# Chunk scans of an RWKV-7 layer: inverses a batch ahead from small products of their own, two heads per masked product, undecayed state, fixed order

## The chip, the core and the metric

The kernel runs on one core of a Trainium2 chip. TensorE (PE in the profile, its weight loads PEld) multiplies matrices out of SBUF into PSUM, VectorE (DVE), ScalarE (ACT) and GpSimd (POOL) work on tiles, and SyncE (SP) issues most of the DMAs. The metric is the device time of one execution in microseconds (us).

## The reference

One encoder layer over 1024 tokens of width 1024, in float32: a norm and one wide projection; banded attention with 8 query heads; an RWKV-7 time mix with 8 heads of 64, as a forward and a backward scan whose outputs are added; gates, an output projection, and a feed-forward part. The scan is what the change is about:

```python
def step(state, inp):
    r_t, w_t, k_t, v_t, a_t, b_t = inp
    sa = jnp.einsum('dbhij,dbhj->dbhi', state, a_t)
    state = (state * w_t[..., None, :] + sa[..., :, None] * b_t[..., None, :]
             + v_t[..., :, None] * k_t[..., None, :])
    y = jnp.einsum('dbhij,dbhj->dbhi', state, r_t)
    return state, y
```

The attention takes 128 queries at a time against three blocks of 128 keys, with a softmax that has one extra logit per head.

## The kernel before

The scan is done by chunks: 16 chunks of 64 tokens (NCH), two directions (ND, the backward one takes the chunks from the end), 8 heads, which lie as four pairs (NP) of two heads in 128 partitions, and two groups of four heads (g). The stage ahead of attention writes to DRAM, for each direction and chunk, `ra_d` (for each head 64 columns of the decayed a and 64 of the decayed r) and `bk_d` (64 columns of b and 64 of k, with b first for the forward direction), and `v_d`.

For one chunk and direction, `products` (L869) multiplies bk by ra for each head, which gives a 128x128 matrix, and masks it into `gm` on VectorE. The rows of b against the columns of a are a strictly triangular 64x64 matrix L, and the scan needs the inverse of I - L. A batch is four chunks (NB), so 4 x 8 heads x 2 directions, 64 matrices. `inverse` (L892) does their 32x32 diagonal blocks at once on VectorE: transposes into `Lp`, then 31 pairs of a multiplication into `tmp` and an addition into `Z`, then two transposes into `Zn` and `Zt`; ScalarE puts these back into `gm`. `inverse_off` (L925) makes the off-diagonal blocks with 32x32 matmuls (`qps`) and puts them into `gm` as well. `gm` has two batches, in turn.

A step of the scan (one chunk, both directions) is then a chain: `w_part` (L979: `wps`, from v and from the old state `Sb`), a copy to `Wt`, `u_part` (L997: `ups`, the inverse times Wt), a copy to `UV`, `s_part` (L1006: `sps`, the state sums; `Tc` is the sum with the decayed old state `Sc`, and `Sb` is Tc times the decay `Dt` of the chunk), beside it `operands` (L957) for the next step, which transposes bk (`tmps`) into `tm`, and `y_part` (L1025: `yps`, the outputs).

What stands on TensorE between these is filler: `gates(0)` in the stages ahead of the scan (384 matmuls `gmm` of 128x512), and `beside` (L747: `gates(1)`, 384 more of the same, then the attention's up-projection, `uaps`) in the scan. `fill(n)` (L776) issues n matmuls of it, and the tables `FILL` and `WARM` say how many at which place; `ahead` says which later chunks' `products` go into which step. Only the masked products and the first matmul of the off-diagonal blocks are held in the order of the program. Everything else is put in an order by the framework's scheduler when the kernel is built: on each engine by the priority of the program's order and by when the scheduler takes an operand to be ready. That order is then fixed, and an engine that comes to an instruction whose operand is late waits.

The first four chunks' products, the first inverse and the first off-diagonal blocks come ahead of the first step. The attention (L674 to L735) is ahead of the scan: scores `sc` for a head, mask and maximum (`smk`), exponential on ScalarE, a scaling on VectorE (L718), transposes of the scores (`pt`, L721), copies to `pT`, and the output product `po` (L729).

## Time and profile before

| | |
|---|---|
| median of 3 runs | 1876.3 us (1874.92 to 1877.21) |
| the profiled execution's own time | 1880.39 us |
| its span | 1878.3 us |
| mean granted TensorE clock | 0.967 |
| attention | about 371 to 497 us of the span |
| chunk scans | about 498 to 938 us |

The profile is of one execution, and its times count from the start of the span. A busy matmul is longer in the records than its share of the stream, since the matmuls are pipelined: the distance from one start to the next says what one costs. fp32 matmuls stand in the trace twice, as two passes; in the listings of the order they stand once.

### The profile page before, as it was taken

How to read it: one execution, taken by the hardware profiler on the slowest of the kernel's cores; microseconds unless marked ns; L12 is line 12 of the kernel's file. 1: busy time of each engine (PE TensorE's matmuls, PEld its weight loads, DVE VectorE, ACT ScalarE, POOL GpSimd, SP SyncE). 2: the span in 40 equal slices, each digit the busy share in tenths (PEclk: the TensorE clock that was granted, in tenths of full speed). 3: DMA queues.
4: the chain of work that ended last, by engine and by line, in shares of the span. 5: the costliest groups of instructions: out<-in, count | busy, mean ns of one | idle time of the engine just before them, and what ended most of it. 6: DMA issues, size and time to landing. Idle time of an engine off the chain costs nothing.

```text
span 1878.3 us, 30687 instructions
## 1 busy us (share of the span) xinstructions
PE 1751.7 (93%) x11800; PEld 1409.7 (75%) x11800; DVE 1206.6 (64%) x2086; ACT 790.6 (42%) x1447; POOL 353.5 (19%) x330
## 2 busy tenths in 40 slices
PE   7999888989996999999978989999999999999998
PEld 7977666756675666666757987788787888888998
DVE  6646776667365668577795277676765786685432
ACT  5536666455423132314562144443443444454221
POOL 3444444521321122133243000000000000000000
PEclk9999999999998889999999999999999999999999
DMA  6362434752462444466557213545345984564111
GB/s 202 91 173 88 141 119 141 215 163 85 124 202 87 151 137 141 149 192 189 158 179 238 83 57 116 169 144 160 129 155 190 308 262 138 185 214 137 60 40 46
DMA packets 259603, 279.74 MB, mean 149 GB/s; under 512 B 15744, under 2 KB 178432, under 8 KB 259328
## 3 DMA queue, kind: packets, MB, share of 16 engines
q1 hardware_dynamic: 251200, 264.46, 44.7%
q0 software_dynamic: 7824, 12.59, 2.4%
q8 instruction: 93, 1.52, 0.3%
q10 hardware_dynamic: 432, 0.73, 0.1%
q14 instruction: 54, 0.44, 0.1%
HBM read 196.97 MB, written 80.74 MB: 148 GB/s over the span
## 4 chain that ended last, share of the span: by engine, by line
PE 40%; DVE 17%; DMA 6%; issue 4%; ACT 2%; SPq 1%; POOL 0%; DVEq 0%; POOLq 0%; ACTq 0%
PE ff2ps L1549 16%; DMA w1st<-in_w_ff_dram 4%; DVE w1l L175 2%; DVE Z L913 2%; PE ff1ps L1309 2%; DVE tmp L910 2%; PE plps L211 2%; PE plps L210 2%; PE plps L209 2%; PE gps L883 2%; PE mmo L209 2%; PE mmo L211 2%; PE mmo L210 2%; DVE h L1326 1%; DVE Sb L1021 1%
## 5 line engine op out<-in xcount | busy, mean ns | idle before, releaser
L175 POOL TENSOR_TENSOR wlo<-wst,whi 128x512 fp32r<-128x512 f32 (+1 forms) x116 | 182.1, 1583 | 332.6 <-ACT whi L174 316.1
L1549 PE MATMUL ff2ps<-th,sh 128*128 128x512 f32 x448 | 174.1, 390 | 3.6 <-ACT th L174 3.6
L1549 PE MATMUL ff2ps<-th,sl 128*128 128x512 f32 x448 | 175.2, 391 | 0.0
L1549 PE MATMUL ff2ps<-tl,sh 128*128 128x512 f32 x448 | 175.1, 391 | 0.0
L162 POOL TENSOR_TENSOR rstd<-ms,neghalf 128x1 f32<-128x1 f32 x24 | 13.3, 554 | 813.5 <-DVE ms L160 813.5
L174 ACT CAST whi<-wst 128x512 fp32r<-128x512 f32 (+1 forms) x116 | 73.5, 649 | 118.3 <-PE gmm L199 48.0
L174 ACT CAST sh<-sst 128x512 fp32r<-128x512 f32 x109 | 67.8, 622 | 113.5 <-PE ff2ps L1549 64.4
L197 PE MATMUL gmm<-hh,whi 128*128 128x512 f32 x256 | 110.1, 430 | 1.6 <-ACT gth L271 1.6
L201 PE MATMUL gmm<-hh,wlo 128*128 128x512 f32 x256 | 109.6, 428 | 0.0
L199 PE MATMUL gmm<-hl,whi 128*128 128x512 f32 x256 | 109.5, 428 | 0.0
L175 DVE TENSOR_TENSOR sl<-sst,sh 128x512 fp32r<-128x512 f32 x109 | 75.2, 689 | 52.2 <-ACT sh L174 51.7
L1549 PEld LDWEIGHTS ff2ps<-th,sh 128*128 128x128 f32 x448 | 84.2, 188 | 21.6 <-ACT th L174 4.1
L1549 PEld LDWEIGHTS ff2ps<-tl,sh 128*128 128x128 f32 x448 | 84.5, 189 | 18.0 <-DVE tl L175 0.2
L1549 PEld LDWEIGHTS ff2ps<-th,sl 128*128 128x128 f32 x448 | 84.5, 189 | 17.5
L886 DVE TENSOR_TENSOR gm<-gps,gmask 128x512 f32<-128x512 f32 x64 | 42.0, 685 | 61.5 <-PE gps L883 59.2
L209 PE MATMUL mmo<-whi,mh 128*128 128x256 f32 x256 | 73.2, 287 | 3.4 <-ACT mh L174 3.4
L209 PE MATMUL plps<-wg,hp 128*128 128x256 f32 x256 | 73.5, 287 | 0.0
L211 PE MATMUL mmo<-whi,ml 128*128 128x256 f32 x256 | 72.7, 286 | 0.2 <-DVE ml L175 0.2
L174 ACT CAST w1h<-w1st 128x512 fp32r<-128x512 f32 x48 | 29.2, 615 | 103.1 <-DMA w1st<-in_w_ff_dram 102.5
L210 PE MATMUL mmo<-wlo,mh 128*128 128x256 f32 x256 | 72.5, 284 | 0.0
L211 PE MATMUL plps<-wg,hp 128*128 128x256 f32 x256 | 72.5, 283 | 0.0
L210 PE MATMUL plps<-wg,hp 128*128 128x256 f32 x256 | 72.4, 283 | 0.0
(379 smaller groups left out, 4992.2 us busy)
## 6 DMA issues: line engine op xcount, KB each, us to landing
wst<-in_w_in_dram SPq DMA_DIRECT2D x92, 256.0 KB, 3.3
tst<-in_w_ff_dram SPq DMA_DIRECT2D x80, 256.0 KB, 3.9
w1st<-in_w_ff_dram SPq DMA_DIRECT2D x32, 512.0 KB, 5.2
hid_S<-h SPq DMA_DIRECT2D x64, 256.0 KB, 2.1
sst<-hid_S SPq DMA_DIRECT2D x64, 256.0 KB, 2.8
hid_A<-h SPq DMA_DIRECT2D x48, 256.0 KB, 2.0
sst<-hid_A SPq DMA_DIRECT2D x45, 256.0 KB, 3.7
ra_d<-ra SPq DMA_DIRECT2D x8, 1024.0 KB, 4.5
```

Of the source, the lines that this page charges most:

```text
L174: a = nc.scalar.copy(hi, src)
L175: b = (lo_eng or nc.vector).tensor_tensor(out=lo, in0=src, in1=hi.bitcast(F32), op=ALU.subtract)
L197: nc.tensor.matmul(ps, ah, bh, start=(i == 0), stop=False)
L199: nc.tensor.matmul(ps, ah, bl, start=False, stop=False)
L201: nc.tensor.matmul(ps, al, bh, start=False, stop=(i == n - 1))
L209: nc.tensor.matmul(ps, ah, bh, start=(i == 0), stop=False)
L210: nc.tensor.matmul(ps, ah, bl, start=False, stop=False)
L211: nc.tensor.matmul(ps, al, bh, start=False, stop=(i == n - 1))
L883: nc.tensor.matmul(pss[q][:, j, :], b_[rows, j, :], r_[rows, j, :], start=True, stop=True))
L886: nc.vector.tensor_tensor(out=gm[b % 2][d][:, ci, q::2, :], in0=pss[q], in1=gmask[:, d, :].unsqueeze(1).broadcast_to([P, NP, P]), op=ALU.mult)
L910: nc.vector.tensor_tensor(out=tv, in0=Lp[:, t + 1:32, t:t + 1].broadcast_to([P, n, m]), in1=Z[:, t:t + 1, 0:m].broadcast_to([P, n, m]), op ...
L1549: nc.tensor.matmul(banks[bs][i], x_[:, isl], y_, start=fresh and p + j == 0, stop=p == NPR - 1 and j == 2, skip_group_check=True)
```

## The change

Six things are changed.

1. Small products of their own. `low_products` loads the 64 columns of a (`la`) and of b (`lb`) of each chunk and makes L alone (`lps`, 64x64), ScalarE copies it to `lt`, and `inverse` starts from that: four ScalarE copies to `Lc`, one transpose of 128x1024 in place of four of 32x1024, the same 31 pairs. The result goes into tiles of its own, `zi`, two batches in turn, and `gm` keeps one batch.
2. A batch ahead. The first batch's low products, inverse and off-diagonal blocks are put into the attention (the latter after its fifth block of queries), and the result goes through DRAM (`zi_d`). Batch 1 has its low products in the prologue and its inverse beside steps 0 to 2; batches 2 and 3 have their low products in steps 3 and 7 and their inverse beside the three steps that follow. Half of the scalings of the scores go from VectorE to ScalarE.
3. Two heads per masked product. `rm` holds ra of a pair twice, with the other head's 64 rows zero, so that one matmul of 128x128 by 256 columns gives both heads, in place of two of 64 rows and 128 columns. `rm` is loaded as two DMAs of 64 rows and has one buffer per direction.
4. Products two steps ahead, two calls a step; two chunks in the prologue.
5. Undecayed state. `Sb` is a copy of the sum (half on VectorE, half on ScalarE); the decay goes into the next chunk's `rac` on ScalarE. `Wt` has zero halves, so that `u_part` contracts over 128 rows; its copies are split between VectorE and ScalarE. PSUM has one bank for each of `wps`, `ups`, `sps` and `yps`, for both groups.
6. Fixed order. All matmuls of the scan, the filler's too, stay in the order of the program, in portions of 9, 9 and 15 fillers a step, 24 in the prologue and 8 between the halves of the off-diagonal blocks; `WARM` is gone.

```diff
-FILL = (96, 2, 0, 2, 7, 12, 6)
-WARM = (1, 1, 3)
+FILL0 = 24
+FILL = (9, 9, 15)
+FILLQ = 8
+QOFF_AT = 4
...
+    def mmo(*a, **kw):
+        tc.keep_in_program_order(nc.tensor.matmul(*a, **kw))
...
+    def zi_tile(pl, name):
+        z = pl.tile([P, 32, 64], F32, name=name, bufs=1)
+        nc.gpsimd.memset(z[32:64, :, 0:32], 0.0)
+        nc.gpsimd.memset(z[64:96, :, 32:64], 0.0)
+        return z
+    def low_products(pl, ps_of, b, mm):
+        lt = pl.tile([P, 32, 64], F32, name="lt", bufs=1)
+        for ci in range(NB):
+            s = NB * b + ci
+            la, lb = ([pl.tile([P, NP, 64], F32, name=n, bufs=2) for _ in range(ND)] for n in ("la", "lb"))
+            for d in range(ND):
+                nc.sync.dma_start(la[d], ra_d[d, chunk(s, d)][:, :, 0:64])
+                nc.sync.dma_start(lb[d], bk_d[d, chunk(s, d)][:, :, 64 * d:64 * d + 64])
+            pss = [ps_of([P, NP, 64], "lps") for _ in range(2)]
+            for j in range(NP):
+                for q in range(2):
+                    for d in range(ND):
+                        e = q ^ d
+                        rows = slice(64 * e, 64 * e + 64)
+                        l_, r_ = (lb, la) if d == 0 else (la, lb)
+                        mm(pss[e][own[d], j, :], l_[d][rows, j, :], r_[d][rows, j, :], start=True, stop=True)
+            for e in range(2):
+                nc.scalar.copy(lt[:, 8 * ci + e:8 * ci + 8:2, :], pss[e])
+            yield lt
+    def inverse(pl, lt):
+        Lc = pl.tile([P, 32, 32], F32, name="Lc", tag="inv", bufs=3)
+        for r0 in range(0, P, 32):
+            k = r0 // 32 % 2
+            nc.scalar.copy(Lc[r0:r0 + 32].rearrange("s t p -> s p t"), lt[r0:r0 + 32, :, 32 * k:32 * k + 32])
+        Lp = pl.tile([P, 32, 32], F32, name="Lp", tag="inv", bufs=3)
+        nc.vector.transpose(out=Lp, in_=Lc)
+        Z = pl.tile([P, 32, 32], F32, name="Z", tag="inv", bufs=3)
+        nc.gpsimd.memset(Z, 0.0)
+        nc.gpsimd.memset(Z.rearrange("p r c -> p (r c)")[:, ::33], 1.0)
...
+        Zn = pl.tile([P, 32, 32], F32, name="Zn", tag="inv", bufs=3)
+        Zt = pl.tile([P, 32, 32], F32, name="Zt", tag="inv", bufs=3)
+        nc.vector.transpose(out=Zn.rearrange("r p c -> r c p"), in_=Z.rearrange("p r c -> p c r"))
+        nc.vector.transpose(out=Zt.rearrange("c p r -> c r p"), in_=Z)
+        return Zn, Zt
+    def inverse_off(pl, ps_of, lt, zz, zi, mm, between):
+        Zn, Zt = zz
+        g = [slice(32 * k, 32 * k + 32) for k in range(4)]
+        Q = pl.tile([P, 32, 32], F32, name="Q", tag="inv", bufs=3)
+        qss = [ps_of([P, 16, 32], "qps") for _ in range(2)]
+        for i in range(32):
+            for r in (0, 2):
+                mm(qss[i // 16][g[r + 1], i % 16, :], lt[g[r], i, 32:64], Zn[g[r], i, :], start=True, stop=True)
+        for hp, qs in enumerate(qss):
+            for r in (1, 3):
+                nc.scalar.copy(Q[g[r], 16 * hp:16 * hp + 16, :], qs[g[r]])
+        for r0, src_ in ((0, Zt), (32, Zt), (64, Zn), (96, Zn)):
+            k = r0 // 32 % 2
+            nc.scalar.copy(zi[r0:r0 + 32, :, 32 * k:32 * k + 32], src_[r0:r0 + 32])
+        between()
+        qss = [ps_of([P, 16, 32], "qps") for _ in range(2)]
+        for i in range(32):
+            mm(qss[i // 16][g[0], i % 16, :], Q[g[1], i, :], Zt[g[1], i, :], start=True, stop=True)
+            mm(qss[i // 16][g[3], i % 16, :], Zt[g[3], i, :], Q[g[3], i, :], start=True, stop=True)
+        for hp, qs in enumerate(qss):
+            nc.scalar.copy(zi[g[0], 16 * hp:16 * hp + 16, 32:64], qs[g[0]])
+            nc.scalar.copy(zi[g[3], 16 * hp:16 * hp + 16, 0:32], qs[g[3]])
...
+        def ps_att(shape, name):
+            return PA.tile(shape, F32, name=name, tag="tp", bufs=3)
+        zi0 = zi_tile(BI0, "zi")
+        lt0 = list(low_products(BI0, ps_att, 0, nc.tensor.matmul))[0]
+        zz0 = inverse(BI0, lt0)
...
-                    nc.vector.tensor_scalar_mul(sm[:, h, 0:nk * P], sm[:, h, 0:nk * P], es[:, h:h + 1])
+                    if h % 2:
+                        nc.scalar.activation(out=sm[:, h, 0:nk * P], in_=sm[:, h, 0:nk * P], func=AF.Copy, scale=es[:, h:h + 1])
+                    else:
+                        nc.vector.tensor_scalar_mul(sm[:, h, 0:nk * P], sm[:, h, 0:nk * P], es[:, h:h + 1])
...
+            if n == QOFF_AT:
+                inverse_off(BI0, ps_att, lt0, zz0, zi0, nc.tensor.matmul, lambda: None)
+                nc.sync.dma_start(zi_d, zi0)
...
+    rms = [BP.tile([P, 2, NP, P], F32, name=f"rm{i}") for i in range(2)]
...
     def products(s, d):
+        c = chunk(s, d)
+        rm = rms[d]
+        for q in range(2):
+            nc.sync.dma_start(rm[own[q], q], ra_d[d, c][own[q]])
         b_ = BP.tile([P, NP, P], F32, name="bkp", bufs=2)
         nc.sync.dma_start(b_, bk_d[d, c])
-        pss = [PB.tile([P, NP, P], F32, name="gps", tag="gps", bufs=2) for _ in range(2)]
-        for j in range(NP):
-            for q in range(2):
-                rows = slice(q * 64, q * 64 + 64)
-                tc.keep_in_program_order(
-                    nc.tensor.matmul(pss[q][:, j, :], b_[rows, j, :], r_[rows, j, :], start=True, stop=True))
-            fill(WARM[1])
-        for q in range(2):
+        for h in range(2):
+            ps = ps_gps([P, 2, 2, P], "gps")
+            for j in range(2):
+                mmo(ps[:, j], b_[:, 2 * h + j, :], rm[:, :, 2 * h + j, :], start=True, stop=True)
             nc.vector.tensor_tensor(
+                out=gm[d][:, s % NB, 4 * h:4 * h + 4, :], in0=ps.rearrange("p j q t -> p (j q) t"),
+                in1=gmask[:, d, :].unsqueeze(1).broadcast_to([P, 4, P]), op=ALU.mult)
...
+            if s > 0:
+                for j in range(NP):
+                    nc.scalar.activation(out=r_[:, j, :], in_=r_[:, j, :], func=AF.Copy, scale=Dt[:, d, j, s - 1:s])
...
+    def wa_part(s):
+        wp = PB.tile([P, 2, 4, 64], F32, name="wps", bufs=1)
+        for g in range(2):
+            for h in range(4):
+                for d in range(ND):
+                    mmo(wp[own[d], g, h, :], gm[d][:, s % NB, 4 * g + h, 0:64], ch_uv[s, g][:, d, h, :],
+                        start=g + h == 0, stop=s == 0, skip_group_check=True)
+        return wp
+    def wb_part(s, wp):
+        for g in range(2):
+            if s > 0:
+                for q in range(2):
+                    for d in range(ND):
+                        mmo(wp[own[d], g, 2 * q:2 * q + 2, :], ch_ra[s, d][:, 2 * g + q, 0:64], Sb[g][1 - s % 2][:, d, q, :, :],
+                            start=False, stop=True, skip_group_check=True)
+            nc.vector.tensor_copy(Wt[g][own[0], 0], wp[own[0], g])
+            nc.scalar.copy(Wt[g][own[1], 1], wp[own[1], g])
+    def u_part(s):
+        up = PB.tile([P, 2, 4, 64], F32, name="ups", bufs=1)
+        for g in range(2):
+            for h in range(4):
+                for d in range(ND):
+                    mmo(up[own[d], g, h, :], zi[s // NB % 2][:, 8 * (s % NB) + 4 * g + h, :], Wt[g][:, d, h, :], start=True, stop=True)
+            UV = ch_uv[s, g]
+            nc.vector.tensor_copy(UV[own[0], 0], up[own[0], g])
+            nc.scalar.copy(UV[own[1], 1], up[own[1], g])
...
+            Tc = sp[:, g]
+            if s > 0:
+                Tc = B.tile([P, ND, 2, 64], F32, name=f"Tc{g}")
+                nc.vector.tensor_tensor(out=Tc, in0=sp[:, g], in1=Sc[g], op=ALU.add)
+            S2 = Sb[g][s % 2]
+            nc.scalar.copy(S2[own[0], :, :, 0, :], Tc[own[0]])
+            nc.vector.tensor_copy(S2[own[1], :, :, 1, :], Tc[own[1]])
+            if s < NCH - 2:
+                Sc[g] = B.tile([P, ND, 2, 64], F32, name=f"Sc{g}", bufs=2)
+                (nc.gpsimd if s > 0 else nc.vector).tensor_tensor(out=Sc[g], in0=Tc, in1=dec, op=ALU.mult)
...
+    lows[1] = low_products(BI, ps_gps, 1, mmo)
+    operands(0)
+    for s in range(2):
         for d in range(ND):
             products(s, d)
-    inverse(0)
-    operands(0)
-    fill(FILL[0])
-    inverse_off(0)
+            low(1)
+            fill(FILL0 // 4)
+    zzs[1] = inverse(BI, lts[1])
+    wb_part(0, wa_part(0))
     ep = None
     for s in range(NCH):
-        b, ci = divmod(s, NB)
-        todo = [(t, d) for t in ahead.get(s, ()) for d in range(ND)]
-        def between(k):
-            for _ in range(min(2 if len(todo) > 2 else 1, len(todo))):
-                products(*todo.pop(0))
-            fill(FILL[k + (0 if s < NCH // 2 else 3)])
-        Wts = [w_part(s, g) for g in range(2)]
-        between(1)
-        for g in range(2):
-            u_part(s, g, Wts[g])
-            fill(WARM[0])
-        between(2)
-        if s < NCH - 1:
-            for g in range(2):
-                s_part(s, g)
+        more = s + 2 < NCH
+        b = s // NB + 2 if s % NB == NB - 1 else None
+        if b is not None and b * NB < NCH:
+            lows[b] = low_products(BI, ps_gps, b, mmo)
+        if more:
+            products(s + 2, 0)
+        low(b)
+        fill(FILL[0] if more else 2 * FILL[0])
+        u_part(s)
+        if s + 1 < NCH:
             operands(s + 1)
-        for g in range(2):
-            y_part(s, g)
-        between(3)
-        if s in (1, 4, 8):
-            inverse({1: 1, 4: 2, 8: 3}[s])
-        if ci == NB - 1 and s + 1 < NCH:
-            inverse_off(b + 1)
+        low(b)
+        fill(FILL[1])
+        if s + 1 < NCH:
+            s_part(s)
+        y_part(s)
+        wp = wa_part(s + 1) if s + 1 < NCH else None
+        low(b)
+        if more:
+            products(s + 2, 1)
+        low(b)
+        fill(FILL[2] if more else 2 * FILL[2])
+        if b in lows:
+            zzs[b] = inverse(BI, lts[b])
+        if s % NB == 2 and s // NB < 3:
+            end_inverse(s // NB + 1)
         if s == 11:
             sBI.close()
             epi["E"] = pool(sE, "epi")
             ep = epilogue(0)
         for _ in range(EPS_AT[s - 12] if s > 11 else 0):
             next(ep)
+        if s + 1 < NCH:
+            wb_part(s + 1, wp)
```

How the change moves instructions shows in the order on two engines. TensorE in the middle of a step, before, from the state's share of `wps` to the triangular solve `ups` (gmm are fillers, gps the masked products):

```order
L990 MATMUL wps<-Sb_4393,rac 64x128 x4
L883 MATMUL gps<-rap,bkp 128x128 x2
L201 MATMUL gmm<-hh_90,wlo 128x512
L883 MATMUL gps<-rap,bkp 128x128 x2
L197 MATMUL gmm<-hh_90,whi 128x512
L883 MATMUL gps<-rap,bkp 128x128 x2
L199 MATMUL gmm<-hl_91,whi 128x512
L883 MATMUL gps<-rap,bkp 128x128 x2
```

And now (L199 is the helper mmo; six more fillers are left out at the dots):

```order
L199 MATMUL wps<-Sb_4737,rac 64x128 x4
L199 MATMUL wps<-Sb_4739,rac 64x128 x4
L199 MATMUL gps<-rm_4743,bkp 128x256 x4
L199 MATMUL gmm<-hh_91,whi 128x512
L199 MATMUL gmm<-hl_92,whi 128x512
L199 MATMUL gmm<-hh_91,wlo 128x512
...
L199 MATMUL ups<-Wt_4741,zi_4730 64x64 x8
L199 MATMUL ups<-Wt_4742,zi_4730 64x64 x8
L1014 MATMUL tmps<-ident,bkc 128x128 x8
```

A call of products is one run of four matmuls with no filler inside, and a run of fillers follows it.

TensorE at the start of the attention, before, up to the first transpose of scores:

```order
L703 MATMUL sc<-kT,qT 128x384 x2
L201 MATMUL gmm<-hh_92,wlo 128x512
L197 MATMUL gmm<-hh_92,whi 128x512
L199 MATMUL gmm<-hl_93,whi 128x512
L201 MATMUL gmm<-hh_92,wlo 128x512
L197 MATMUL gmm<-hh_92,whi 128x512
L721 MATMUL pt<-ident,smk 128x128 x6
```

And now, the last low block and the first transpose:

```order
L205 MATMUL gmm<-hh_93,whi 128x512
L712 MATMUL lps<-la,lb 64x64
L207 MATMUL gmm<-hl_94,whi 128x512
...
L712 MATMUL lps<-lb,la 64x64
L712 MATMUL lps<-la,lb 64x64
L712 MATMUL lps<-lb,la 64x64
L827 MATMUL pt<-ident,smk 128x128 x2
```

All four low blocks of the first batch stand ahead of the first transpose, and with them more fillers: 268 of the 384 in place of 220. All 384 stand ahead of the attention's last output product, where 339 did.

VectorE, before, at the end of an inverse in the loop (gm are the masks):

```order
L910 TENSOR_TENSOR tmp<-Lp,Z 128x31
L913 TENSOR_TENSOR Z<-Z,tmp 128x31
L916 STREAM_TRANSPOSE Zn<-Z 128x32x32
L917 STREAM_TRANSPOSE Zt<-Z 128x32x32
L994 COPY Wt_6299<-wps 128x256
L994 COPY Wt_6314<-wps 128x256
L886 TENSOR_TENSOR gm_4387<-gps,gmask 128x4x128 x2
```

And now:

```order
L1055 COPY UV_6421<-ups 64x256
L732 TENSOR_TENSOR tmp<-Lp,Z 128x31
L735 TENSOR_TENSOR Z<-Z,tmp 128x31
L738 STREAM_TRANSPOSE Zn<-Z 128x32x32
L739 STREAM_TRANSPOSE Zt<-Z 128x32x32
L1068 TENSOR_TENSOR Tc_6669<-sps,Sc_6448 128x256
L1071 COPY Sb_4738<-Tc_6669 64x4x64
```

In place of the copies to Wt, the state sum of a step stands right behind the inverse's last two transposes. Between the masks of a direction and that Tc stand 31 of the inverse's operations, two transposes, four masks and four copies.

More of the change, by code (lines that the diff above doesn't have):

```diff
@@ L1039, in y_part, with low @@
             if s < NCH // 2:
-                nc.scalar.copy(yo, yp[:, d])
+                nc.scalar.copy(yo, yp[:, :, d])
             else:
-                nc.vector.tensor_tensor(out=yo, in0=yo, in1=yp[:, d], op=ALU.add)
-    ahead = {0: (4, 5), 1: (6, 7), 2: (8, 9), 3: (10,), 4: (11,), 6: (12, 13), 7: (14,), 8: (15,)}
-    for s in range(NB):
+                nc.vector.tensor_tensor(out=yo, in0=yo, in1=yp[:, :, d], op=ALU.add)
+    lts, zzs, lows = {}, {}, {}
+    def low(b):
+        if b in lows:
+            lts[b] = next(lows[b])
```

212 lines of the change are left out of this document (67 added, 145 removed).

## The prediction

> **What bounds the kernel now.** I read the page's engine totals first, then the span cut into stages by the view of windows, then the groups by line inside the two stages that the change touches, and last the order in time on TensorE inside one step of the scan. Columns of a window row: its length, busy time and instructions of PE, PEld, DVE, ACT, POOL, the granted clock, DMA share, GB/s.
>
> ```profile
> PE 1751.7 (93%) x11800; PEld 1409.7 (75%) x11800; DVE 1206.6 (64%) x2086; ACT 790.6 (42%) x1447; POOL 353.5 (19%) x330
> ...
> 370.00:498.00 128.00, 119.72 (x573) 76.70 (x573) 85.20 (x291) 70.30 (x208) 26.51 (x27) 0.98 0.37 112
> 498.00:540.00 42.00, 36.35 (x224) 27.97 (x222) 11.04 (x16) 6.84 (x12) 14.09 (x20) 0.92 0.72 225
> 540.00:570.00 30.00, 27.43 (x124) 22.13 (x122) 28.58 (x43) 8.53 (x15) 12.21 (x9) 1.00 0.53 166
> 570.00:580.00 10.00, 0.00 (x0) 0.00 (x0) 9.14 (x26) 0.00 (x0) 0.00 (x0) 0.62 0.09 26
> 580.00:598.00 18.00, 16.24 (x338) 13.35 (x339) 4.70 (x6) 10.00 (x14) 1.30 (x1) 0.74 0.11 32
> 598.00:645.00 47.00, 43.09 (x506) 31.81 (x507) 30.19 (x54) 8.61 (x22) 9.79 (x16) 0.95 0.58 180
> 645.00:700.00 55.00, 51.27 (x640) 37.33 (x639) 37.12 (x80) 16.69 (x33) 11.82 (x17) 0.79 0.42 129
> 700.00:800.00 100.00, 93.62 (x1481) 67.97 (x1479) 68.91 (x140) 31.20 (x66) 23.32 (x38) 1.00 0.46 142
> 800.00:900.00 100.00, 92.08 (x1132) 67.43 (x1133) 72.30 (x147) 30.29 (x52) 32.13 (x40) 0.97 0.65 198
> 900.00:940.00 40.00, 38.08 (x622) 28.85 (x621) 32.85 (x71) 23.07 (x40) 8.39 (x15) 1.00 0.46 137
> ```
>
> Attention is the first row; the chunk scans run from 498 to 938. TensorE is busy over 90% nearly everywhere, so both stages are its own, with one hole: 570 to 580, where only VectorE works, on the first batch's inverse. The clock falls there and again in 645 to 700. From 598 to 940, TensorE idles 3.91 + 3.73 + 6.38 + 7.92 + 1.92 = 23.9 us, with 5.7 more in 498 to 540.
>
> **The change part by part.** *Products.* In time on TensorE (start, length, line, count; starts give the cadence, since lengths overlap):
>
> ```profile
> 602.86 0.49 PE L883 MATMUL gps<-rap,bkp 64*128 64x128 f32 x4
> 603.28 0.49 PE L199 MATMUL gmm<-hl,whi 128*128 128x512 f32 x1
> 603.70 0.49 PE L883 MATMUL gps<-rap,bkp 64*128 64x128 f32 x4
> 604.12 0.49 PE L201 MATMUL gmm<-hh,wlo 128*128 128x512 f32 x1
> ...
> 605.63 1.09 PE L967 MATMUL tmps<-ident,bkc 128*128 128x128 f32 x8
> 606.65 0.69 PE L1036 MATMUL yps<-gm,UV 128*64 128x64 f32 x16
> 607.27 0.50 PE L197 MATMUL gmm<-hh,whi 128*128 128x512 f32 x1
> 607.60 0.40 PE L199 MATMUL gmm<-hl,whi 128*128 128x512 f32 x1
> 607.84 0.40 PE L201 MATMUL gmm<-hh,wlo 128*128 128x512 f32 x1
> ...
> 608.78 1.16 PE L883 MATMUL gps<-rap,bkp 64*128 64x128 f32 x16
> 609.87 0.50 PE L197 MATMUL gmm<-hh,whi 128*128 128x512 f32 x1
> ...
> 619.75 0.68 PE L1002 MATMUL ups<-Wt,gm 64*64 64x64 f32 x16
> 620.36 0.50 PE L199 MATMUL gmm<-hl,whi 128*128 128x512 f32 x1
> ```
>
> An unbroken call is 16 instructions in 608.78 to 609.87, 1.09. Broken by a filler after every quarter it takes 0.42 per quarter and 0.42 per filler, 3.36; apart they would be 1.09 + 4 x 0.24 = 2.05 (0.24: 607.60 to 607.84). So breaking a call costs 1.31. In the trace 56 of the quarters that follow 593 stand so, 14 calls: 18 us, which the change removes. A call then becomes 8 instructions of 128 rows by 256 columns, which the trace lacks. Above, it would be 8 x 2 x 0.128 = 2.0 by the 128-column transposes (8 in 605.63 to 606.65, 0.128 each); below, 1.09, if doubling the rows in one pass were free. I take 2.0, since the transposes have its shape and type: 32 x 0.9 = +29. Net +11. The masks (two of 128x512) stay. The Trainium skill, TensorEngine Tiling (Array Packing), Key Properties, says that a change of tiling mode drains TensorE; the slowed fillers agree. Its Theoretical Speedup, up to 2x for a contraction of at most 64, speaks against the change: the masked products give that factor up, as the row of transposes also says.
>
> *Low products.* Each of 16 chunks gets 32 new instructions of 64x64 by 64. The first-triangular solves are that shape: 16 in 0.61, so 1.22, and 1.3 with a switch. Four blocks go into attention (+5, counted there), 12 into the scan: +15.5.
>
> *Attention.*
>
> ```profile
> L721 PE MATMUL pt<-ident,smk x176: 270/273/369, 388.2 to 493.4; 128*128 128x128 f32 x176
> ...
> L718 DVE TENSOR_SCALAR smk<-smk,es 128x384 f32<-128x384 f32 (+1 forms) x64 | 29.8, 521 | 0.4
> ...
> L902 DVE STREAM_TRANSPOSE Lp<-gm x16: 1952/2064/2274, 538.0 to 817.1; 32x1024 f32<-32x1024 f32 x16
> ...
> L910 DVE TENSOR_TENSOR tmp<-Lp,Z x124: 191/364/1435, 547.8 to 864.5; 128x31 f32<-128x31 f32 x8, 128x60 f32<-128x60 f32 x8, 128x87 f32<-128x87 f32 x8, 128x112 f32<-128x112 f32 x8
> L913 DVE TENSOR_TENSOR Z<-Z,tmp x124: 191/359/1500, 548.7 to 864.7; 128x31 f32<-128x31 f32 x8, 128x60 f32<-128x60 f32 x8, 128x87 f32<-128x87 f32 x8, 128x112 f32<-128x112 f32 x8
> ...
> L936 PE MATMUL qps<-Zn,gm 32*32 32x32 f32 x256 | 14.7, 215 | 17.0 <-DVE Zn L916 17.0
> ```
>
> Attention's pace begins with its first transpose of scores, at 388.2. By the two orders 220 filler matmuls stood ahead of it and now 268 do, 48 x 0.24 = 11.5, and the four low blocks, 5.2, whose loads can add 0.5: +17. Behind it 119 fillers become 116 (-0.7), and the first batch's off-diagonal products come in. One batch of these is 256 instructions; 6.5 by the 32x32 rows at about 25 ns. VectorE gets one inverse, about 62 x 0.42 + 3 x 2.1 = 32, and loses 32 scalings of 0.52 = 17 to ScalarE, which also gets the copies: 100 of some 150 us on VectorE and about 105 on ScalarE, both under TensorE. I take nothing more for their queues (0 to 8). The stage ends 23 us later, near 521. But all 384 fillers are then done, where 45 were left: -10.8 in the scan, and -6.5 for the products that moved, -17.
>
> *The first inverse.* 2.6 + 10.0 us of idle TensorE in 540 to 580, and the tail into 580: -13. The loads of prologue products two to four now fall into the loop, beside fillers.
>
> *The clock.* 18 x 0.26 + 55 x 0.21 + 47 x 0.05 + 42 x 0.08 = 22 us were lost to it. Fillers in fixed portions (9, 9, 15 a step) keep TensorE fed; I take 20 back (0 to 22).
>
> *State.* The decay leaves VectorE's path between a step's state sums and the next step's first product: Sb as one copy each on VectorE and ScalarE. That is 2 x 0.6 us a step by its row below, but under fillers both before and now: nothing on the path. The scaling of rac (8 of 128x128 a step on ScalarE, about 0.3 each by the ScalarE copy of Q, 0.58 for 32x512) has some 13 us of a 19 us step free. With the cover gone it would cost 2.4 a step.
>
> ```profile
> L1021 DVE TENSOR_TENSOR Sb<-Tc,Dt x56: 406/423/1471, 626.8 to 926.1; 64x256 f32<-64x256 f32 x56
> L942 ACT COPY Q<-qps x8: 577/577/578, 585.2 to 883.1; 32x512 f32<-32x512 f32 x8
> L994 DVE COPY Wt<-wps x32: 410/418/426, 594.2 to 931.5; 128x256 f32<-128x256 f32 x32
> L886 DVE TENSOR_TENSOR gm<-gps,gmask 128x512 f32<-128x512 f32 x64 | 42.0, 685 | 61.5 <-PE gps L883 59.2
> ...
> UV<-v_d SPq DMA_DIRECT2D x64, 64.0 KB, 3.6
> rap<-ra_d SPq DMA_DIRECT2D x30, 256.0 KB, 2.8
> ```
>
> *Waits that the fixed order brings.* TensorE in the scan cannot go round a late operand any more. (a) After attention no filler is left over the first loads, which land 2.8 to 3.6 us after issue, two deep: 7. (b) la and lb hold one chunk, so the next chunk's four loads issue on SP only when a low block is done, and the fourth block of a batch stands one product call (2.0) behind the third: about 2 us a time, 8 in all. Queued behind that block are the fillers, and behind them the state. (c) In an inverse VectorE's queue, from the masks to the next step's Tc, holds 31 inverse operations (11), Zn and Zt (4.1), four masks (2.7) and four copies (1.7): 19.6, against 13.7 of TensorE from the same products to the state sums. Part is made up in the step ahead; 2.3 each, 7. (d) The last two steps: 4. Together 26 (15 to 50) against 29.6 of idling that stands there now: -3.5.
>
> Sum: +23 - 17 - 13 - 20 + 11 + 15.5 - 3.5 = -4, so 1876.4 on the profiled execution's own 1880.39 (span 1878.3). That one lies 4.1 above the median of the three runs shown; on the median it is **1872 us**.
>
> **The rivals.** *Faster by far, 1846.* The fixed order leaves TensorE no wait but the start: 26 becomes 12, the clock is whole (-2), attention hides the low loads and part of the fillers ahead of its first transpose (+13 for +23). -4 - 14 - 2 - 10 = -30. For it: the present order already keeps 94% with scattered fillers. Against: attention is at 119.72 of 128 already, so what is put in lengthens it.
>
> *Slower: VectorE sets the pace wherever an inverse runs, 1895.* The place is (c): 19.6 against 13.7 means 6 lost in the second step and 2 in the first, three times, 24 for 7, and 6 in attention, where transposes already waited 5.7 us for VectorE's scalings. -4 + 17 + 6 = +19. It decides once VectorE needs over about 16 us between those masks and Tc. For: today's 540 to 580 shows the inverse taking all of VectorE. Against: three steps lie between an inverse and its use.
>
> *Slower: the low products wait for their loads, 1900.* If each of the 12 blocks in the scan meets a load that has just been issued, 12 x 3 = 36 for 8: -4 + 28 = +24. It decides if SP holds those loads behind a load whose buffer is not yet free. For: one chunk's buffers; against: only the fourth block stands close behind its predecessor. Every row of la is 256 bytes; the Trainium skill, DMA: Bandwidth & Descriptors, Specifications, puts line rate at 512 bytes or more, which would make this rival likelier. The nearest transfer here, 64 KB of UV, took 3.6 us against 2.8 for four times the bytes, in 1 KB rows.
>
> *The switches stay, 1890.* Low blocks and solves bring as many borders as the broken calls had: the 18 is not gained, -4 + 18 = +14. The order has about eight borders a step, and I counted only one.
>
> **How the numbers follow.** The forecast's case has 0.45, with a range of its own of 1859 to 1885 (attention 15 to 31, clock, waits, added as independent); the fast one 0.18, VectorE 0.17, the loads 0.12, the switches 0.08. For the whole, 1843 to 1902. Under 0.2% (4 us) a measurement of this kernel tells nothing from no change. The forecast's case splits 0.25, 0.11 and 0.09 into faster, same and slower; with the fast rival, and 0.04 of same spread over the slower ones, it makes 0.43, 0.15 and 0.42.
>
> **What would show it.** No idle stretch of TensorE over 5 us after attention; granted clock 0.97 or more through the scan; attention's last output product near 519 and the last scan product near 932; product calls of 2.0 us unbroken, low blocks of 1.3; TensorE's waits in the scan naming lps by DMA (8 us) and sps or wps by VectorE (7 us). I am wrong if attention ends past 530 or before 512, if calls take 1.1, or if a low block waits 3 us each time.

## The result

| | median, us | against the kernel before (95% interval) |
|---|---|---|
| before | 1875.6 | |
| changed | 1986.3 (1982.1 to 1987.8) | 1.0585 (1.0562 to 1.0608) |

The change costs 111 us. The forecast was 1872, with a range up to 1902: the time went the other way, and far past the range.

The view of windows gives the loss by stage. Its columns are the window, its length, busy time and instructions of PE, PEld, DVE, ACT, POOL, the granted clock, DMA share and GB/s. The boundaries are each kernel's own: attention's first transpose of scores, its end, the first product of the first step, the last output product. Before:

```profile
371.00:388.00 17.00, 15.20 (x73) 12.01 (x71) 5.72 (x27) 6.31 (x19) 6.75 (x7) 1.00 0.92 288
388.00:497.00 109.00, 102.52 (x496) 63.16 (x495) 79.20 (x265) 63.72 (x190) 18.76 (x18) 0.98 0.28 83
497.00:593.00 96.00, 76.81 (x619) 60.92 (x619) 51.42 (x84) 23.88 (x40) 28.61 (x32) 0.88 0.52 161
593.00:937.00 344.00, 319.35 (x4433) 234.25 (x4428) 240.46 (x487) 109.38 (x210) 85.44 (x123) 0.95 0.52 159
```

After:

```profile
371.00:412.00 41.00, 35.39 (x253) 26.43 (x251) 8.30 (x31) 16.02 (x43) 14.66 (x14) 0.91 0.72 204
412.00:534.00 122.00, 107.48 (x749) 68.13 (x744) 87.67 (x293) 92.02 (x227) 25.70 (x29) 0.98 0.28 85
534.00:575.00 41.00, 23.38 (x196) 16.34 (x196) 5.53 (x8) 6.41 (x14) 5.34 (x12) 0.79 0.76 211
575.00:1042.00 467.00, 367.41 (x4688) 293.59 (x4689) 217.18 (x439) 203.24 (x417) 97.57 (x133) 0.90 0.49 144
```

Attention is 37 us longer (17 + 109 to 41 + 122), the prologue 55 shorter, the loop of the steps 123 longer: 105, and the spans differ by 107. In the loop TensorE's idle time went from 344 - 319.4 = 24.7 us to 467 - 367.4 = 99.6, that is +75. Its busy time grew by 48, of which an estimated 39 are 162 fillers that stood in the prologue before (at 0.24 each, their distance from start to start). The scan as a whole, prologue and loop, is 68 longer and idles 73 longer. The loss there is waiting, not work. What TensorE waited for most in the loop (who, for whom, us in total, times, the longest), before and after:

```profile
PE yps L1034 <- DVE y L1042: 8.0, 6, 4.0
PE gps L883 <- DVE gm L886: 4.6, 4, 2.7
PE qps L936 <- DVE Zn L916: 3.7, 1, 3.7
```

```profile
PE wps L199 <- ACT Wt L1046: 34.5, 14, 4.9
PE ups L199 <- ACT UV L1056: 18.1, 15, 2.9
PE sps L199 <- DVE Tc L1068: 13.7, 14, 2.7
PE gps L199 <- ACT lt L714: 8.5, 2, 4.4
PE uaps L199 <- ACT wuhi L178: 7.8, 1, 7.8
```

Three kinds, once in nearly every step, make 66 us, and they have an odd form: `wps` waits for a copy out of `wps`, `ups` for a copy out of `ups`. The order in time at one of them, in a step with an inverse, on TensorE, VectorE and ScalarE (start, length, instruction, idle time before it):

```profile
723.28 0.66 PE L199 MATMUL wps<-Sb,rac 128*64 128x128 f32 x8
728.45 1.12 PE L199 MATMUL wps<-Sb,rac 128*64 128x128 f32 x8 [4.52 <-ACT Wt L1046]
...
723.58 1.36 DVE L732 TENSOR_TENSOR tmp<-Lp,Z 128x240 f32<-128x240 f32 x1
724.98 1.35 DVE L735 TENSOR_TENSOR Z<-Z,tmp 128x240 f32<-128x240 f32 x1
...
727.53 0.41 DVE L1045 COPY Wt<-wps 64x256 f32<-64x256 f32 x1
...
728.03 0.37 ACT L1046 COPY Wt<-wps 64x256 f32<-64x256 f32 x1 [4.02 <-DVE Wt L1045]
```

The first group's eight records, four matmuls of two passes, end at 723.9. VectorE comes to its copy at 727.53, behind pieces of the inverse, ScalarE copies after VectorE, and only then does TensorE begin the second group. In most steps without an inverse the second group of `wps` waits 0.9 to 1.2 us, that of `ups` about 1.0 and that of `sps` 0.6. Beside an inverse `wps` waits 3.1 to 4.9 us, five times, together 20 of its 34.5. Yet the second group needs nothing of these copies: it adds to its own half of the PSUM tile. The built program has the wait in it. The two groups' first matmuls in one step, with the engines they wait for:

```
L199 MATMUL wps<-Sb_4737,rac 64x128 [waits DVE_49,Activation_49]
L199 MATMUL wps<-Sb_4737,rac 64x128 x3
L199 MATMUL wps<-Sb_4739,rac 64x128 [waits Activation_49]
L199 MATMUL wps<-Sb_4739,rac 64x128 x3
```

What the two groups share is one PSUM bank (part 5 of the change). The Trainium skill, PSUM — Partial Sum Buffer, section PSUM bank collisions raise a hardware error, says that two engines must not use one bank and quadrant of partitions at once, whichever bytes they touch and reads included, and that software has to keep them apart. The trace agrees in that the framework orders them: TensorE after ScalarE (34.5 us), ScalarE after VectorE (37.6 us of waiting for the copies to `Wt`, below). By that section of the Trainium skill the two copies, on different quadrants, could overlap. Here they don't. It is not because both write one tile: the two copies to `Sb`, which read one tile of SBUF and write one tile of SBUF, can start together:

```profile
643.00 0.29 DVE L1071 COPY Sb<-Tc 64x256 f32<-64x256 f32 x1
643.00 0.41 ACT L1070 COPY Sb<-Tc 64x256 f32<-64x256 f32 x1 [2.07 <-DVE Tc L1068]
```

The two groups share a PSUM tile and with it the bank, and the edits below part both at once. So the runs don't tell whether the waits go by tile or by bank, and whether the chip needs any of them was not tried.

### The profile page after: what moved, and what is told of

Its sections match the earlier page's. It is cut to its first block, busy times and chain, and to the rows that moved or that the text cites. A ratio compares the mean times of both kernels' runs of the same rounds, so it can differ in the third digit from the quotient of the medians.

```text
span 1985.3 us, 31536 instructions
## 1 busy us (share of the span) xinstructions
PE 1776.4 (89%) x12056; PEld 1447.1 (73%) x12056; DVE 1149.2 (58%) x1996; ACT 905.8 (46%) x1693; POOL 356.0 (18%) x338
## 4 chain that ended last, share of the span: by engine, by line
PE 58%; DVE 16%; DMA 10%; ACT 7%; issue 5%; POOL 2%; SPq 1%; DVEq 0%; POOLq 0%; ACTq 0%
PE ff2ps L1614 15%; DMA w1st<-in_w_ff_dram 4%; PE gps L199 3%; PE ff1ps L1374 2%; PE gmm L199 2%; PE uaps L199 2%; DVE w1l L179 2%; ACT Lc L722 2%; PE plps L219 2%; PE plps L218 2%; PE plps L217 2%; PE po L835 2%; PE mmo L217 1%; PE mmo L218 1%; PE mmo L219 1%
## 5 line engine op out<-in xcount | busy, mean ns | idle before, releaser
L199 PE MATMUL gps<-rm,bkp 128*128 128x256 f32 x256 | 78.1, 458 | 10.2 <-ACT lt L714 8.5
L199 PEld LDWEIGHTS gps<-rm,bkp 128*128 128x128 f32 x256 | 55.6, 227 | 23.0 <-ACT lt L714 8.8
L179 DVE TENSOR_TENSOR w1l<-w1st,w1h 128x512 fp32r<-128x512 f32 x48 | 32.8, 689 | 50.7 <-ACT w1h L178 50.7
```

What stands on the lines that cost most here:

```text
L179: b = (lo_eng or nc.vector).tensor_tensor(out=lo, in0=src, in1=hi.bitcast(F32), op=ALU.subtract)
L199: tc.keep_in_program_order(nc.tensor.matmul(*a, **kw))
```

## Experiments: which part costs it

Theory B is that shared bank. Theory A is ScalarE's queue, which now has the copies behind a scaling of rac that waits for its load (40.0 us in the loop):

```profile
ACT UV L1056 <- DVE UV L1055: 46.0, 15, 6.0
ACT rac L1009 <- DMA rac<-ra_d: 40.0, 13, 5.6
ACT Wt L1046 <- DVE Wt L1045: 37.6, 22, 4.0
```

Theory W is the added work on TensorE. The first four kernels are the changed one with one edit each.

**Banks per group.**

```diff
-        wp = PB.tile([P, 2, 4, 64], F32, name="wps", bufs=1)
+        wp = [PB.tile([P, 4, 64], F32, name="wps", tag="ch", bufs=3) for _ in range(2)]
...
-        up = PB.tile([P, 2, 4, 64], F32, name="ups", bufs=1)
         for g in range(2):
+            up = PB.tile([P, 4, 64], F32, name="ups", tag="ch", bufs=3)
...
+            sp = PB.tile([P, ND, 2, 64], F32, name="sps", tag="ch", bufs=3)
```

> The changed kernel, with wps, ups and sps again in PSUM tiles of one group each (three tiles in turn), so that the two groups of heads no longer share a bank; all else as changed. Theory B (shared bank: a group's matmuls wait until VectorE and then ScalarE have copied the other group out of the same bank; 34.5 + 18.1 + 16 us of TensorE's idle time in the loop, and some 20 us of granted clock with it): about 1900 us. Theory A (ScalarE's queue: the scaling of rac waits 40 us for its loads with the copies of Wt, UV and Sb behind it): about 1965 us. Theory W (the added work on TensorE, not waits): within 10 us of 1986.

1914.8 us, 1.0221 (1.0181 to 1.0261): 71.5 us less than the change, 15 short of theory B's figure and far from the others. None of the three kinds stands in the list of its waits any more. For `ups` the list has these:

```profile
PE ups L199 <- ACT Wt L1046: 5.3, 4, 2.9
PE ups L199 <- DVE Wt L1045: 3.5, 4, 1.5
```

They are waits of the chain itself: `Wt` is the copy that `ups` multiplies.

**Copies behind both groups**, in the shared bank:

```diff
             if s > 0:
...
+        for g in range(2):
             nc.vector.tensor_copy(Wt[g][own[0], 0], wp[own[0], g])
             nc.scalar.copy(Wt[g][own[1], 1], wp[own[1], g])
```

(and so for `ups`).

> The changed kernel, banks as changed, but the matmuls of both groups come first and the copies of both groups behind them (in the products for Wt and for UV; the state sums stay as they are). Theory B: the waits of wps and ups between the groups go (53 us and part of the clock), sps stays: about 1920 us. Theory A: the copies stand as late on ScalarE as before: about 1980 us. Theory W: 1986.

1936.5 us, 1.0336 (1.0300 to 1.0372): 50 less than the change, with the bank still shared. The waits of `wps` for Wt and of `ups` for UV are gone, and the one that was left in stays, `sps`:

```profile
PE sps L199 <- DVE Tc L1070: 18.0, 14, 2.9
```

**The decay back on the state**, rac unscaled:

```diff
-                for j in range(NP):
-                    nc.scalar.activation(out=r_[:, j, :], in_=r_[:, j, :], func=AF.Copy, scale=Dt[:, d, j, s - 1:s])
...
-            nc.scalar.copy(S2[own[0], :, :, 0, :], Tc[own[0]])
-            nc.vector.tensor_copy(S2[own[1], :, :, 1, :], Tc[own[1]])
+            for q in range(2):
+                nc.vector.tensor_tensor(out=S2[own[q], :, :, q, :], in0=Tc[own[q]], in1=dec[own[q]], op=ALU.mult)
```

> The changed kernel, with the decay back on the state (two multiplications on VectorE per group) and rac unscaled, so that ScalarE never waits for a load of rac and loses 2.4 us of work a step. Theory A: about 1930 us. Theory B: the ScalarE part of each hop is sooner now and then, about 1965 us. Theory W: 1986.

1985.7 us, 1.0599 (1.0535 to 1.0663): no gain. ScalarE no longer waits for rac, and TensorE waits as before:

```profile
PE wps L199 <- ACT Wt L1042: 31.0, 14, 4.6
PE ups L199 <- ACT UV L1052: 21.7, 15, 3.7
PE sps L199 <- DVE Tc L1064: 14.2, 14, 2.8
```

**All copies on VectorE.**

```diff
-            nc.scalar.copy(Wt[g][own[1], 1], wp[own[1], g])
+            nc.vector.tensor_copy(Wt[g][own[1], 1], wp[own[1], g])
...
-            nc.scalar.copy(UV[own[1], 1], up[own[1], g])
+            nc.vector.tensor_copy(UV[own[1], 1], up[own[1], g])
...
-            nc.scalar.copy(S2[own[0], :, :, 0, :], Tc[own[0]])
+            nc.vector.tensor_copy(S2[own[0], :, :, 0, :], Tc[own[0]])
```

> The changed kernel, with the ScalarE halves of the copies to Wt, UV and Sb moved to VectorE; banks, order and scaled rac as changed. Theory A: no copy stands behind ScalarE's loads any more, about 1920 us. Theory B: the hop stays and one engine change in it goes, about 1960 us. Theory W: 1986.

1988.7 us, 1.0615 (1.0572 to 1.0657): no gain again, and above the figures of A and B alike. The same waits now name VectorE:

```profile
PE ups L199 <- DVE UV L1056: 28.3, 15, 5.8
PE wps L199 <- DVE Wt L1046: 28.0, 14, 5.1
PE sps L199 <- DVE Tc L1068: 17.7, 14, 4.1
```

Theory A has fallen: the hop costs as much with whichever engine makes it, and so has B's small gain from one engine less. The four together show the hop between the groups.

## Experiments: what is left, and why the bank is so dear

With banks per group 41 us are left against the kernel before. Theory C puts them into attention, theory D into waits that a fixed order cannot go round. Three edits on top of that kernel, and one on the kernel before, tell.

**The decay back on the state** (the diff as above), on banks per group.

> The kernel with banks per group (1915 us) and with the decay back on the state, rac unscaled. With the shared bank this edit gave nothing. Theory A2 (once the bank is free, ScalarE's 43 us of waiting for rac's loads delay the copies): about 1895 us. Theory C (what is left of the loss lies in attention, which ends at 529 instead of 497): within 6 us of 1915. Theory D (what is left are waits that the fixed order cannot go round, in the loop): within 8 of 1915.

1908.4 us, 1.0160 (1.0101 to 1.0219), 6 us less than without; the intervals overlap.

**The first batch out of the attention.**

```diff
-        lt0 = list(low_products(BI0, ps_att, 0, nc.tensor.matmul))[0]
-        zz0 = inverse(BI0, lt0)
...
+    lt0 = list(low_products(BI, ps_gps, 0, mmo))[0]
+    zz0 = inverse(BI, lt0)
     operands(0)
...
+    fill(72)
+    inverse_off(BI, ps_gps, lt0, zz0, zi[0], mmo, lambda: fill(FILLQ))
```

(and the low blocks of batch 1, with their fillers, stand behind that).

> Banks per group, and the first batch's low products, inverse and off-diagonal blocks out of the attention again: they stand at the start of the scan, with 72 more fillers in the prologue for cover. Theory C: attention ends 25 to 30 us sooner, the prologue gets the work on TensorE (5 + 6.5) and some 8 us of the inverse uncovered: about 1903 us. Theory D: the two cancel or worse, 1915 to 1930.

1930.2 us, 1.0276 (1.0217 to 1.0336): 15 us more by the medians, 10 by the ratios to the kernel before, and the intervals overlap. Attention's last output product starts at 494.5 instead of 529.5, but the first step's first product at 609.3 instead of 570.1. Part of that is the edit's own: its low blocks stand one behind the other, and wait for their loads:

```profile
PE lps L199 <- DMA lb<-bk_d: 31.8, 16, 8.1
```

So theory C, which had 12 us less, has fallen: the 35 us by which attention is longer buy at least what they cost, against this arrangement.

**No matmul of the scan held in the order of the program.**

```diff
     def mmo(*a, **kw):
-        tc.keep_in_program_order(nc.tensor.matmul(*a, **kw))
+        nc.tensor.matmul(*a, **kw)
...
-                tc.keep_in_program_order(nc.tensor.transpose(tp[:, q, :], b_[:, q, :], ident))
+                nc.tensor.transpose(tp[:, q, :], b_[:, q, :], ident)
```

> Banks per group, and no matmul of the scan held in the order of the program: the scheduler places them. Theory D: about 1895 us, waits for loads and casts in the loop are gone round. Theory C: within 8 of 1915, or slower where products are broken up by fillers again.

1886.0 us, 1.0046 (1.0019 to 1.0074): 29 less than banks per group in fixed order. TensorE's idle time fell from 15 to 2 us between attention's last output product and the first step's first product, and from 59 to 38 in the loop. So theory D holds, and not in the loop alone.

**The kernel before, with its calls of products unbroken.**

```diff
-            fill(WARM[1])
+        fill(4 * WARM[1])
```

(out of the loop over j).

> The kernel before, with one edit: the four fillers of a call of products stand behind the call instead of one behind every quarter. By the term of the prediction (14 broken calls of 1.31 us each) 18 us less, about 1857 us; if the slowed fillers and quarters only fill time in which TensorE would wait, no change.

1872.4 us, 0.9976 (0.9952 to 0.9999): 4 us where the prediction's term had 18. In the trace 14 of the 32 calls still have one break, behind their first pair, so a part of the 18 stays. In the loop TensorE's busy time fell by 13 us, and its idle time rose by 5.

Then the free order alone, in the shared bank.

> The changed kernel with its shared banks and no matmul of the scan held in the order of the program. Theory E (bank and fixed order multiply: what makes the shared bank dear is that no filler can slip between the two groups): the scheduler fills the hops, most of the 71 us come back, about 1920 us. Theory F (they add): the 29 us that the free order gave with banks per group, about 1957 us.

1900.2 us, 1.0117 (1.0077 to 1.0158): 86 us less than the change. This makes a table, as ratios to the kernel before:

| | fixed order | free order |
|---|---|---|
| shared bank | 1.0585 | 1.0117 |
| banks per group | 1.0221 | 1.0046 |

Either edit alone takes back most of the loss, so the two do not add: each is dear because of the other. The order of the free kernel shows how. Between the two groups of `wps` and of `ups` the scheduler has put a call's products, transposes and fillers (rows left out at the dots):

```
L199 MATMUL wps<-Sb_4737,rac 64x128 x4
L199 MATMUL gps<-rm_4743,bkp 128x256 x3
L199 MATMUL wps<-Sb_4739,rac 64x128 x4
...
L199 MATMUL ups<-Wt_4741,zi_4733 64x64 x8
L1014 MATMUL tmps<-ident,bkc 128x128 x8
L199 MATMUL gmm<-hh_91,wlo 128x512
L199 MATMUL gmm<-hh_91,whi 128x512
L199 MATMUL gmm<-hl_92,whi 128x512
L199 MATMUL ups<-Wt_4742,zi_4733 64x64 x8
```

The waits of the first two kinds fell from 52.6 us to 20.8:

```profile
PE wps L199 <- ACT Wt L1046: 12.8, 7, 3.4
PE ups L199 <- ACT UV L1056: 8.0, 3, 4.3
```

To see whether it is this and not something else that the scheduler did, the same was written by hand, in fixed order and shared bank:

```diff
         if more:
             products(s + 2, 0)
+        if s > 0:
+            wb_part(s, wp, (1,))
...
-        u_part(s)
+        u_part(s, 0)
         if s + 1 < NCH:
             operands(s + 1)
         low(b)
-        fill(FILL[1])
+        fill(4)
+        u_part(s, 1)
+        fill(FILL[1] - 4)
         if s + 1 < NCH:
-            s_part(s)
-        y_part(s)
+            s_part(s, 0)
+        y_part(s, 0)
+        if s + 1 < NCH:
+            s_part(s, 1)
+        y_part(s, 1)
...
-            wb_part(s + 1, wp)
+            wb_part(s + 1, wp, (0,))
```

(the parts now take the groups that they do).

> The changed kernel, its shared banks and its fixed order kept, but the second group's matmuls stand a piece of other work behind the first group's: a product call between the two halves of wps, the transposes tmps and four fillers between the two of ups, the first group's outputs between the two of sps. Nothing is added or taken away. Theory E (the shared bank costs because nothing stands between the groups while VectorE and ScalarE copy): most of the 70 us come back, about 1925 us. If instead the bank itself is slow to hand from engine to engine: above 1960 us.

1946.6 us, 1.0385 (1.0301 to 1.0470): 40 us less, with the same instructions, banks and pinning. That is two thirds of what was expected: no wait of `ups` or `sps` is left among the larger ones, while `wps` still waits, probably because one call of products (1.64) does not cover the hop behind an inverse:

```profile
PE wps L199 <- ACT Wt L1046: 20.3, 10, 3.0
```

## Experiments: the products, and the fastest version

**Products as pairs of 64-row matmuls again**, unbroken, first on the free order with banks per group, then on the changed kernel alone:

```diff
-            ps = ps_gps([P, 2, 2, P], "gps")
-            for j in range(2):
-                mmo(ps[:, j], b_[:, 2 * h + j, :], rm[:, :, 2 * h + j, :], start=True, stop=True)
...
+        pss = [ps_gps([P, NP, P], "gps") for _ in range(2)]
+        for j in range(NP):
+            for q in range(2):
+                tc.keep_in_program_order(
+                    nc.tensor.matmul(pss[q][:, j, :], b_[own[q], j, :], r_[own[q], j, :], start=True, stop=True))
```

(with one load of ra, and masks to match).

> Banks per group, free order (1886 us), and the products again as pairs of 64-row matmuls, unbroken, two PSUM tiles by head. Theory G (the call's own time on TensorE, 1.65 us from start to start in the changed kernel against 1.09, is on the path): 32 x 0.56 = 18 us less, about 1868 us. If the calls lie under waits: within 6 of 1886.

1884.8 us, 1.0034 (1.0011 to 1.0057), against 1.0046: the two cannot be told apart.

> The changed kernel, with only the products as pairs of 64-row matmuls again. Theory G: 18 us less than 1986, about 1968 us, if TensorE's own time counts beside the waits of the shared bank; within 6 of 1986 if those waits hide it.

1981.1 us, 1.0548 (1.0522 to 1.0574): 5 us, and here too the intervals overlap. A call of the masked kind takes 1.64 from start to start in the changed kernel:

```profile
753.88 2.00 PE L199 MATMUL gps<-rm,bkp 128*128 128x256 f32 x8
755.52 0.59 PE L199 MATMUL gmm<-hh,wlo 128*128 128x512 f32 x1
```

So theory G, that this time is on the path, has fallen too: 32 x 0.55 = 18 us of TensorE's time are worth 1 to 5. Where the 18 us went shows in part. In the loop of the free kernel TensorE's busy time fell by 10 us and its idle time rose by 8. And the mean granted clock over all executions was 0.961 with row-tiled products where it was 0.969 with masked ones, and 0.940 where it was 0.951 in the shared bank. By an estimate from these figures the lower clock is worth 0.008 of 1885 us, 15 us, in the free kernel. Whether it follows from the lighter load was not tried.

**The fastest version**: the free order, banks per group, row-tiled products, the decay on the state, and two chunks of buffers for the low products:

```diff
-            la, lb = ([pl.tile([P, NP, 64], F32, name=n, bufs=2) for _ in range(ND)] for n in ("la", "lb"))
+            la, lb = ([pl.tile([P, NP, 64], F32, name=n, bufs=4) for _ in range(ND)] for n in ("la", "lb"))
```

> As the last, with the decay back on the state (it gave 6 us beside the banks per group) and two chunks of buffers for la and lb in place of one (waits for lb are 4.6 in the scan and 4.3 in attention, and some of the 17 us before attention's first transpose): about 1856 us, 1 per cent faster than the kernel before. If attention's end, 31 us later, is made of TensorE's work alone: about 1863 us.

1865.3 us, 0.9946 (0.9921 to 0.9970): half a per cent under the kernel before, and 19.5 us under the free kernel with row-tiled products. Two kernels split that.

> The fastest kernel so far (banks per group, free order, row-tiled products, decay on the state, two chunks of buffers for la and lb: 1865 us) with the undecayed state again. It tells the share of the buffers from that of the decay in the 20 us between the two. If the buffers carried it (attention's first transpose went from 408.6 to 396.6): about 1870 us; if the decay did: about 1880 us.

1877.8 us, 1.0017 (0.9989 to 1.0045): without the decay on the state 13 us are lost. The buffers would then have given 7, but there the intervals overlap; it lies between the two expectations. Attention's transposes of scores in the two kernels that differ by the buffers alone, without and with two chunks (shortest, median and longest; first and last start):

```profile
L827 PE MATMUL pt<-ident,smk x176: 270/273/478, 408.6 to 528.9; 128*128 128x128 f32 x176
```

```profile
L827 PE MATMUL pt<-ident,smk x176: 270/273/473, 400.0 to 521.5; 128*128 128x128 f32 x176
```

Over all the kernels above with the first batch in the attention, the first transpose starts at 404.8 to 412.0 without the buffers and at 395.6 to 400.0 with them. With the undecayed state ScalarE again waits for rac, 24 us in this kernel.

> The fastest kernel so far with the fixed order of the changed kernel. Theory D (fixed order costs 29 us by its waits for loads and casts, once the banks are apart): about 1892 us. If those waits came from the loads of la and lb, which have more buffers here: about 1870 us.

1883.9 us, 1.0047 (1.0018 to 1.0077): the fixed order costs 19 us even there, between the two expectations.

## Why the prediction was wrong

**The step that failed** is the list of waits that the fixed order brings. It had four entries, 26 us together, and rightly said that TensorE "cannot go round a late operand any more", but took only operands for late. It left out the wait between the two groups through their one bank, although the change's description names the bank, and the built program names the wait. That is 66 us of idle time in the trace. Entry (a), the first loads, was too small as well: in the prologue TensorE waited 10.0 + 4.8 + 1.7 = 16.5 us for loads, where it had 7. With the list fell the term for the clock: 20 us were to come back, and the loop was granted 0.90 instead of 0.95. The lower clock goes with the waiting: with banks per group the loop was granted 0.94.

**Attention**: +23 predicted, +37 measured. The first transpose came 24 later, where the sum had 17. The loads of `la` and `lb` have a part in that: TensorE waited 5.5 us for `lb` there, where 0.5 was counted. But the kernels without the buffers, whose attention is the same, have that transpose at 404.8 to 412.0, 17 to 24 later than before, and the changed kernel stands at the late end. So much of this miss is spread. The rest of the miss lies behind the first transpose: 13 longer, where the sum had 6. TensorE idles 14.5 us there instead of 6.5, and waits for VectorE's scalings and ScalarE's copies, the queues for which "nothing more" was taken. Before and after:

```profile
PE pt L721 <- DVE smk L718: 5.7, 8, 1.2
```

```profile
PE pt L827 <- DVE smk L824: 8.3, 9, 2.7
PE pt L827 <- ACT pT L831: 3.8, 1, 3.8
```

The rival with late low loads had the mechanism of late loads. It placed it in the scan, where it was small: in the loop of the changed kernel TensorE never waits for lb, and in the prologue 4.8 us.

**The first inverse**: that it pays to take it out of the prologue was not contradicted. The kernel with it put back is 10 to 15 us slower, within overlapping intervals, and part of that is the edit's own.

**Products**: the cost of a call, 2.0, was 1.64, and the price of breaking shows in TensorE's busy time, 13 us less in the loop when most breaks are gone. What was wrong is that either was charged to the end: undone alone they gave 4, 1 and 5 us. Busy TensorE at 94% was read as TensorE being the path. By the rule of the Trainium skill that row tiling gives up to 2x (TensorEngine Tiling (Array Packing), Theoretical Speedup), the masked call should be the dearer one. It is, 1.64 against 1.09, but no run shows that in the time. Why removed work gave so little was not settled: that the chain of copies between steps sets the pace instead is argued, not shown, and the lower granted clock beside it is the other candidate.

**State**: "nothing on the path" holds with the shared bank (0 us) and is wrong without it: 6 in one pair, within overlapping intervals, and 13 in another, clear of them. The cover that was named, ScalarE's free time, does not help when the queue stands still for a load: the scalings of rac wait for DMAs (42.8 us with banks per group), and the copies stand behind them. That this is where the 13 us come from is argued.

**VectorE in the inverse**, the rival at 1895, was near in size and wrong in place. Its 24 us were to be lost between the masks and the state sums, on the chain. What the inverse lengthened is the hop between the groups: 20 of the 34.5 us of `wps` stand beside an inverse, and its waits there are 3.1 to 4.9 us instead of mostly 0.9 to 1.2. With banks per group none of these waits is left.

**What had been named to show it**: the clock through the scan (0.97 named, 0.90 in the loop) and the scan's end (932 named, 1042 measured) both told against the forecast at first sight; attention past 530 (534) had been named as a sign of error, and it was, though the smaller part. The list of waits did name `sps` by VectorE, but for 13.7 us and through the bank, where 7 had been expected from the inverse.

Left open: 0.5% of the change that the two edits together do not give back (1.0046), and whether the copies' order after each other could be lifted.

## What to carry to other kernels

When tiles are merged into one PSUM bank, count a wait for each engine that reads one part while TensorE has yet to write the other, and look at the built program's waits for it: data dependence alone does not show it. Such a wait costs what the slowest queue in the hop costs, and it is dear only when nothing stands between; so merging banks and fixing the order are not two separate edits. A TensorE that is busy 94% need not be the path: work that was taken off it here gave well under half of its length.

## What was not expected of the hardware and the framework

A copy of 64x256 on ScalarE waits for VectorE's copy of the other 64 partitions of the same PSUM tile, 37.6 us in the loop, also where each group has its own bank (17.4 us), while the two engines' copies from one SBUF tile can start together. And a call of masked products, 8 records of 128 rows by 256 columns, takes 1.64 us, 0.20 each, less than twice the 0.128 of the 128-column transposes.
